# A hybrid RWKV-7 and delta-net block on one core: substitution and half of the low parts on GpSimd, decays from broadcast sums, one inversion list, and a new order

## The chip, the cores and the metric

The kernel runs on one core of one Trainium2 chip. The metric is the device time of one execution in microseconds. The engines are TensorE (PE, with its weight loads listed apart as PEld), VectorE (DVE), ScalarE (ACT), GpSimd (POOL) and SyncE (SP), whose queue issues most of the DMAs; GpSimd issues some too.

## The reference

One layer over 256 latent tokens and 256 context tokens of width 2048: an adaLN-modulated RMSNorm, one input projection `h @ w_in`, two token mixers side by side, a gated merge, an output projection, and a SwiGLU feed-forward part of hidden size 5632. All of it is fp32. What matters here is the two mixers.

The first is a bidirectional RWKV-7 scan of 16 heads of 64. The second is a bidirectional gated delta net of 8 heads of 128, in chunks:

```python
gc = jnp.cumsum(chunks(g), axis=-1)
diff = gc[..., :, None] - gc[..., None, :]
decay = jnp.where(incl, jnp.exp(jnp.where(incl, diff, 0.0)), 0.0)
lmat = jnp.where(strict, jnp.einsum('nbhik,nbhjk->nbhij', kb, kc) * decay, 0.0)
sol = lax.linalg.triangular_solve(lmat, rhs, left_side=True, lower=True, unit_diagonal=True)
qk = jnp.where(incl, jnp.einsum('nbhik,nbhjk->nbhij', qc, kc) * decay, 0.0)
q_dec = qc * jnp.exp(gc)[..., None]
```

`decay` is a matrix of exponentials of differences of running sums, and the triangular solve is done in the kernel by inverting unit triangular blocks. The RWKV scan is brought into the same chunked form, with its own triangular inverse.

## The kernel before

**Products.** Each fp32 weight is split in two parts that TensorE takes at full rate: ScalarE rounds it to a high part (`whi`), VectorE subtracts that from the weight to get the low part (`wlo`), and TensorE forms high x high, high x low and low x high. In the token stage this is done by `cast` and `products` (pieces of 8 row blocks, split in two halves of 4, so each subtraction has 128x512 elements); outside it by `load_w` and `gemm` (L368 the subtraction, L377 to L379 the three products).

**Stages.** First the modulation and the low-rank columns (to about 120 us). Then the token stage, one function per task: the RWKV pairs (`prepare`, `grams`, `inverse`, `values`, `scan`; eight pairs of heads), and the delta-net heads (`begin` once, then for each head `features`, `tokens`, `decays`, `head_grams`, `head_inverse`, `head_scan`). Weight products for features and gates run between them as filler. Then the merge: two projections of both mixers' outputs (`pa`, `pb`, 16 column blocks each), the output projection (`wout`), and the feed-forward part. Through the heads' stage and the merge, rows of the modulation matrix are summed on VectorE as they arrive (`ada_rest`, `scale2`; L1530), their loads issued by GpSimd.

**The inverse.** `invert` inverts blocks of 64. It writes them to DRAM, reads them back as 16x16 blocks, one to a partition, and solves these by substitution: fifteen steps of one multiplication and one addition, each of 15 to 64 elements on 128 partitions (64 for heads), all on the tile `arena` and each dependent on the last. It writes the result to DRAM, reads it back in block form (`T0`, `Tx`), and joins 16 to 32 and 32 to 64 by small products (`pi` tiles).

**The decays.** `decays(h)` multiplies a triangle of ones by the head's `g` on VectorE (`gm`), sums by a product with the strict triangle `aft`, takes the exponential on ScalarE and masks it on GpSimd (`Ed`). A second product, with `ones`, gives the running sum for the query factor.

**The order.** In the token stage the order on TensorE, VectorE, ScalarE and GpSimd is written out by a planner (`Weave`). Each task hands it one instruction or group at a time; the planner takes the one that can start first by its own costs (the `Lane` constants, `LAT`) and, among equals, by `RANK`. `GATES_A` and `GATES_B` say how many gate products may go after each pair and head. Each engine then works strictly in that order. SyncE's queue holds the loads in the order in which they were handed over.

## Time and profile before

| | before |
|---|---|
| median of 3 runs | 2276.34 us (2275.34 to 2285.3) |
| profiled execution | 2291.02 us |
| its span, first to last instruction | 2289.2 us |
| mean granted TensorE clock | 0.978 |
| token stage | about 120 to 1300 us |
| merge and output projection | about 1300 to 1520 us |
| feed-forward part | about 1520 us to the end |

The three runs are not the profiled execution, which took some 13 us longer; times of single instructions come from that one. In the rows that follow, a group is read as line, engine, operation, output and inputs, shape, count, then busy time in us and the mean of one in ns, then idle time of the engine just before it and what ended that. A helper records nearly all instructions of the token stage, so these have one line (L146) and are told apart by their tiles. A duration of TensorE holds an overlap with the next product.

### The profile page before, as it was taken

To read this page: it belongs to the slowest core of one execution; us is meant where nothing else is said; L and a number is where in the kernel's file an instruction comes from. 1 tells how busy PE (TensorE), PEld (TensorE's weight loads), DVE (VectorE), ACT (ScalarE), POOL (GpSimd) and SP (SyncE) were. 2 spreads that over 40 slices of the span, in tenths; PEclk is the share of its full clock that TensorE was granted. 3 is DMA by queue.
4 is the path that set the end of the run, shared out by engine and by line. 5 is a ranking of instruction groups with operands and counts; after the bars stand their busy time and mean duration, and the time that the engine had idled before them with its cause. 6 is when DMAs were issued, how large, how long until landed. Compare 5 with 4: busy or idle time off the path is not lost. (4 is left out here: it accounts for less than half of the span.)

```text
span 2289.2 us, 53997 instructions
## 1 busy us (share of the span) xinstructions
PE 2191.2 (96%) x22584; PEld 1944.7 (85%) x22584; DVE 1566.3 (68%) x3233; ACT 1068.0 (47%) x1894; POOL 115.2 (5%) x185
## 2 busy tenths in 40 slices
PE   7998999999999999999999989899999999999998
PEld 4766587777878778878889888889999999999997
DVE  3446488778888668888899768774656655545444
ACT  3245555444454455444545464443444444444443
POOL 0000000000000010111101040000000000000000
PEclk9999999989999999999999999999999999999999
DMA  9955544344343436455557777854777776566665
GB/s 388 402 143 166 171 119 131 94 104 108 107 118 107 119 106 190 142 165 157 166 160 251 250 280 266 290 194 144 233 240 235 235 231 213 188 184 192 187 188 162
DMA packets 231924, 430.72 MB, mean 188 GB/s; under 512 B 114944, under 2 KB 129152, under 8 KB 227328
## 3 DMA queue, kind: packets, MB, share of 16 engines
q1 hardware_dynamic: 203744, 350.72, 49.9%
q0 software_dynamic: 14112, 51.39, 7.1%
q10 hardware_dynamic: 13824, 25.17, 3.3%
q8 instruction: 177, 2.90, 0.5%
q14 instruction: 67, 0.55, 0.1%
HBM read 401.44 MB, written 25.77 MB: 187 GB/s over the span
## 5 line engine op out<-in xcount | busy, mean ns | idle before, releaser
L368 DVE TENSOR_TENSOR wlo<-wraw,whi 128x1024 fp32r<-128x1024 f32 x328 | 394.1, 1202 | 329.9 <-ACT whi L367 327.0
L367 ACT CAST whi<-wraw 128x1024 fp32r<-128x1024 f32 x328 | 337.6, 1030 | 478.9 <-PE mm L378 429.2
L146 PE MATMUL mm<-hxh,whi 128*128 128x256 f32 (+1 forms) x1376 | 467.5, 340 | 6.2 <-ACT whi L146 6.0
L146 PE MATMUL mm<-hxh,wlo 128*128 128x256 f32 (+1 forms) x1376 | 465.9, 339 | 4.1 <-DVE wlo L146 3.9
L146 PE MATMUL mm<-hxl,whi 128*128 128x256 f32 (+1 forms) x1376 | 465.7, 338 | 0.0
L379 PE MATMUL mm<-hfh,wlo 128*128 128x256 f32 x1344 | 376.1, 280 | 0.5 <-DVE wlo L368 0.5
L377 PE MATMUL mm<-hfh,whi 128*128 128x256 f32 x1344 | 376.1, 280 | 0.0
L378 PE MATMUL mm<-hfl,whi 128*128 128x256 f32 x1344 | 375.9, 280 | 0.0
L146 PEld LDWEIGHTS mm<-hxh,whi 128*128 128x128 f32 x1376 | 264.3, 192 | 33.9 <-ACT whi L146 7.4
L146 PEld LDWEIGHTS mm<-hxh,wlo 128*128 128x128 f32 x1376 | 264.2, 192 | 31.4 <-DVE wlo L146 6.1
L146 PEld LDWEIGHTS mm<-hxl,whi 128*128 128x128 f32 x1376 | 264.0, 192 | 25.9 <-issue 5.4
L146 DVE TENSOR_TENSOR wlo<-wraw,whi 128x512 fp32r<-128x512 f32 x344 | 236.5, 689 | 68.1 <-ACT whi L146 66.3
L146 ACT CAST whi<-wraw 128x512 fp32r<-128x512 f32 x344 | 205.0, 617 | 112.6 <-PE mm L146 79.0
L379 PEld LDWEIGHTS mm<-hfh,wlo 128*128 128x128 f32 x1344 | 253.2, 188 | 0.9 <-DVE wlo L368 0.9
L377 PEld LDWEIGHTS mm<-hfh,whi 128*128 128x128 f32 x1344 | 253.4, 189 | 0.0
L378 PEld LDWEIGHTS mm<-hfl,whi 128*128 128x128 f32 x1344 | 253.2, 188 | 0.0
L146 DVE TENSOR_TENSOR arena<-arena 128x28 f32<-128x28 f32 (+13 forms) x538 | 133.1, 249 | 23.6 <-DMA arena<-scr 10.5
L377 PE MATMUL mm<-za,whi 128*128 128x256 f32 x512 | 143.3, 280 | 0.0
L379 PE MATMUL mm<-za,wlo 128*128 128x256 f32 x512 | 143.2, 280 | 0.0
L378 PE MATMUL mm<-za,whi 128*128 128x256 f32 x512 | 143.2, 280 | 0.0
L378 PEld LDWEIGHTS mm<-za,whi 128*128 128x128 f32 x512 | 96.4, 188 | 0.0
L379 PEld LDWEIGHTS mm<-za,wlo 128*128 128x128 f32 x512 | 96.4, 188 | 0.0
(320 smaller groups left out, 3978.5 us busy)
## 6 DMA issues: line engine op xcount, KB each, us to landing
wraw<-w SPq DMA_DIRECT2D x172, 512.0 KB, 4.1
wraw<-wgu SPq DMA_DIRECT2D x168, 512.0 KB, 4.4
aw<-ada_rest POOLq DMA_DIRECT2D x96, 512.0 KB, 5.2
aw<-ada_first SPq DMA_DIRECT2D x32, 1024.0 KB, 11.2
wraw<-wdn SPq DMA_DIRECT2D x64, 448.0 KB, 3.7
wraw<-wout SPq DMA_DIRECT2D x32, 512.0 KB, 4.8
aw<-ada_gt ACTq DMA_DIRECT2D x64, 256.0 KB, 4.8
wraw<-wdn SPq DMA_DIRECT2D x32, 512.0 KB, 3.7
```

Source lines behind the costliest of these rows:

```text
L146: return Op(self, cost, lambda: getattr(self.engine, name)(out, *a, **k), kind)
L367: S.copy(hi[:, c, :M], raw[:, c, :M])
L368: V.tensor_sub(lo[:, c, :M], raw[:, c, :M], hi[:, c, :M].bitcast(F32))
L377: E.matmul(ps, hi, Xh[:, k, :n], start=first and i == 0, stop=False)
L378: E.matmul(ps, hi, Xl[:, k, :n], start=False, stop=False)
L379: E.matmul(ps, lo, Xh[:, k, :n], start=False, stop=last and i == len(wt) - 1)
```

## The change

1. **Substitution.** All thirty instructions of each of the sixteen substitutions, and the two fills ahead of them, go to GpSimd. The parameter that chose the engine of the fills is gone.
2. **Low parts.** In the token stage the second half of each piece (128x512) is subtracted on GpSimd, the first half on VectorE. In the merge and the output projection (`side`), where a piece was one subtraction of 128x1024 on VectorE, its first 4 row blocks stay there and the rest goes to GpSimd. The feed-forward part stays as it is.
3. **Decays.** `begin` forms the running sums of `g` in both directions by two scans, stores them to DRAM (`grow`) and transposes them (`gct`). `decays` loads one row to all partitions, subtracts the column on GpSimd, bounds the difference by a mask of 0 and -200 on VectorE (`past`, a new constant) and takes the exponential; the query factor is the exponential of the row itself. Its two products are gone.
4. **Inversion list.** For heads, the second small product of the join runs on quarters of 32x32 (`fours`) rather than on blocks of 64x64.
5. **Order.** New `RANK`, `LAT`, `GATES_A`, `GATES_B` and costs of GpSimd's lane.

```diff
-GATES_A, GATES_B = (6, 2, 3, 4, 0, 1, 4, 3), (2, 3, 0, 1, 1, 0, 9, 1)
+GATES_A, GATES_B = (8, 0, 5, 8, 2, 0, 0, 0), (2, 1, 1, 2, 4, 6, 1, 0)
-LAT = dict(dma=2.04, hop=0.255, own=0.092, grp=32, cg=4, turn=0.17)
+LAT = dict(dma=2.76, hop=0.172, own=0.015, grp=32, cg=4, turn=0.132)
-    g = Lane(G, 0.06, 0.0024, LAT["own"])
+    g = gp = Lane(G, 0.17, 0.0019, LAT["own"])
...
+    put("past", np.where(np.concatenate([u <= v, u >= v], 1), 0.0, -200.0))
...
-                V.tensor_sub(lo[:, c, :M], raw[:, c, :M], hi[:, c, :M].bitcast(F32))
+                for en, d in (((V, c),) if side[0] is V else ((V, slice(c.start, c.start + 4)), (G, slice(c.start + 4, c.stop)))):
+                    en.tensor_sub(lo[:, d, :M], raw[:, d, :M], hi[:, d, :M].bitcast(F32))
...
-            yield v.tensor_mul(pr, X[:nb, j + 1:, j:j + 1].to_broadcast([nb, n, m]),
+            yield g.tensor_mul(pr, X[:nb, j + 1:, j:j + 1].to_broadcast([nb, n, m]),
                                TT[:nb, j:j + 1, :m].to_broadcast([nb, n, m]))
-            yield v.tensor_add(TT[:nb, j + 1:, :m], TT[:nb, j + 1:, :m], pr)
+            yield g.tensor_add(TT[:nb, j + 1:, :m], TT[:nb, j + 1:, :m], pr)
...
+        if nu == 16:
+            yield [e.matmul(pv[64 * h:64 * h + 64, 1, u], Tx[64 * h:64 * h + 64, u, :], Qm[64 * h:64 * h + 64, u, :],
+                            start=True, stop=True) for u in range(nu) for h in range(2)]
+        else:
+            yield [e.matmul(pv[r, 1, u], Tx[r, u, b:b + 32], Qm[r, u, :], start=True, stop=True) for h, u, b, r in fours]
...
-                yield v.tensor_sub(lo[:, g], raw[:, g], hi[:, g].bitcast(F32))
+                yield (gp if k else v).tensor_sub(lo[:, g], raw[:, g], hi[:, g].bitcast(F32))
...
+        yield v.tensor_tensor_scan(t0, ones, sp, 0.0, ALU.mult, ALU.add)
+        yield v.tensor_tensor_scan(t1[:, ::-1], ones, sp[:, ::-1], 0.0, ALU.mult, ALU.add)
+        for d, t in enumerate((t0, t1)):
+            for b in range(4):
+                dq(grow[d, :, P * b:P * b + P], t[32 * b:32 * b + 16])
...
-            gm = gs.tile([P, 4, P], F32, tag="gm", name="gm")
-            yield v.tensor_mul(gm, tri[:, d].unsqueeze(1).to_broadcast([P, 4, P]),
-                               gtok[:, :, col:col + 1].to_broadcast([P, 4, P]))
-            gf = gm.rearrange("p b c -> p (b c)")
-            ps = yield pab
-            yield e.matmul(ps, aft[:, d], gf, start=True, stop=True)
+            row = gs.tile([P, 4, P], F32, tag="row", name="row")
+            yield dq(row.rearrange("p b t -> p (b t)"), grow[d, 8 * d + h, :].partition_broadcast(P))
             ed = gs.tile([P, 4, P], F32, tag=f"Ed{d}", name="Ed")
-            yield s.activation(ed.rearrange("p b c -> p (b c)"), ps, AF.Exp)
-            weave.release(pab)
-            yield g.tensor_mul(ed, ed, tri[:, d].unsqueeze(1).to_broadcast([P, 4, P]))
+            yield g.tensor_sub(ed, row, gct[:, :, col:col + 1].to_broadcast([P, 4, P]))
+            yield v.tensor_tensor(ed, ed, past[:, d].unsqueeze(1).to_broadcast([P, 4, P]), ALU.min)
+            yield s.activation(ed.rearrange("p b c -> p (b c)"), ed.rearrange("p b c -> p (b c)"), AF.Exp)
             Ed.append(ed)
...
-            ps = yield pab
-            yield e.matmul(ps[:, :T], ones, gf[:, 0:T], start=True, stop=True)
-            eq = gs.tile([P, T], F32, tag="eq", name="eq")
-            yield s.activation(eq, ps[:, :T], AF.Exp)
-            weave.release(pab)
-            yield v.tensor_mul(o["Qe"][:, d], o["q"], eq)
+        yield v.tensor_mul(o["Qe"][:, 0], o["q"], first)
+        eq = row[:, 0:2].rearrange("p b c -> p (b c)")
+        yield s.activation(eq, eq, AF.Exp)
+        yield v.tensor_mul(o["Qe"][:, 1], o["q"], eq)
...
     scale_next = scale2()
+    side[0] = G
...
+    side[0] = V
     r = rms_scale(x1p, [ssum, sq], T, "rs")
```

Three places show what moves. Before, a head's substitution stands on VectorE. The numbers 64x60, 64x10x6 and so on are its steps; `Vn` and `St` belong to the scan of another head, `wlo` to a weight:

```order
L146 TENSOR_TENSOR arena<-arena 64x55
L146 TENSOR_SCALAR Vn<-s,btok 128x128
L146 TENSOR_TENSOR arena<-arena 64x11x5
L146 TENSOR_SCALAR Vn<-s,btok 128x128
L146 TENSOR_TENSOR arena<-arena 64x60
L146 TENSOR_TENSOR arena<-arena 64x10x6
L146 TENSOR_TENSOR arena<-arena 64x63
```

Now a head's substitution stands on GpSimd, with issues of modulation rows and low parts between its steps:

```order
L147 TENSOR_TENSOR arena<-arena 64x60
L147 TENSOR_TENSOR arena<-arena 64x6x10
L147 TENSOR_TENSOR arena<-arena 64x55
L125 DMA aw<-ada_rest 128x1024
L147 TENSOR_TENSOR arena<-arena 64x5x11
L125 DMA aw<-ada_rest 128x1024
L147 TENSOR_TENSOR arena<-arena 64x48
L125 DMA aw<-ada_rest 128x1024
L147 TENSOR_TENSOR arena<-arena 64x4x12
```

The chain is the same, and what stands between its steps is now GpSimd's other work instead of VectorE's.

On TensorE, in the heads' stage before, a decays' product with ones (`pa<-arena,C 128x256`) stands among the weight products, ahead of the head's Gram products (`pa<-arena 128x128`):

```order
L146 MATMUL pi<-T_12267,LT 32x32 x16
L146 MATMUL mm<-hxh,wlo 128x512
L146 MATMUL pa<-arena,C 128x256
L146 MATMUL mm<-hxh,whi 128x512
L146 MATMUL mm<-hxl,whi 128x512
L146 MATMUL mm<-hxh,wlo 128x512
L146 MATMUL pi<-Tx,qo 32x32 x16
L146 MATMUL mm<-hxh,whi 128x512
L146 MATMUL mm<-hxl,whi 128x512
L146 MATMUL pa<-arena 128x128 x2
```

Now, at the like place of a head, only weight products stand between the inverse's join and the Gram products:

```order
L147 MATMUL pi<-Tx,qo 32x32 x16
L147 MATMUL mm<-hxh,whi 128x256
L147 MATMUL mm<-hxl,whi 128x256
L147 MATMUL mm<-hxh,wlo 128x256
L147 MATMUL mm<-hxh,whi 128x256
L147 MATMUL pa<-arena 128x128 x2
```

Two products of each direction are gone from there.

On GpSimd in the merge, before, the multiplications of the first projection by its gates (L1578) alternate with issues of rows (L1528):

```order
L1555 DMA gts<-gts__1351 128x4x256
L1578 TENSOR_TENSOR PA<-PA,gts 128x256 x6
L1528 DMA aw<-ada_rest 128x1024 x3
L1578 TENSOR_TENSOR PA<-PA,gts 128x256
L1528 DMA aw<-ada_rest 128x1024
L1578 TENSOR_TENSOR PA<-PA,gts 128x256
```

Now (L1590 and L1539 are the same two lines) a low part of each piece stands between them:

```order
L1590 TENSOR_TENSOR PA<-PA,gts 128x256
L1539 DMA aw<-ada_rest 128x1024
L371 TENSOR_TENSOR wlo<-wraw,whi 128x512
L1590 TENSOR_TENSOR PA<-PA,gts 128x256
L1539 DMA aw<-ada_rest 128x1024
L371 TENSOR_TENSOR wlo<-wraw,whi 128x512
```

Each low part waits for its own weight, and what stands behind it on GpSimd waits with it.

More of the change, by code (lines that the diff above doesn't have):

```diff
@@ L561, in unit_rows, with invert @@
         return bass.AP(a.tensor, a.offset + (2 * u0 + h) * UNIT, [[64, 64], [2 * UNIT, nu], [1, 64]])
-    def invert(pool, Lt, parts, nu, which, full, fill):
+    def invert(pool, Lt, parts, nu, which, full):
         h2 = nu // 2
@@ L675, in emit @@
     btok = cst.tile([P, 4, 16], F32, name="btok")
+    gct = cst.tile([P, 4, 16], F32, name="gct")
+    grow = dpool.tile([2, 16, 512], F32, name="grow")
     egc = cst.tile([P, 4, 16], F32, name="egc")
@@ L1163, in begin @@
         sp, bet, t0, t1 = (l2s[:, i:i + P] for i in range(0, 512, P))
[L1164 removed]
+        t2 = gs.tile([P, 512], F32, tag="row", name="t2")[:, 0:P]
         yield dq(sp, abd.rearrange("b r t -> (b r) t"))
@@ L1309, in decays @@
-            eq = gs.tile([P, T], F32, tag="eq", name="eq")
-            yield s.activation(eq, ps[:, :T], AF.Exp)
-            weave.release(pab)
-            yield v.tensor_mul(o["Qe"][:, d], o["q"], eq)
+                first = gs.tile([P, T], F32, tag="eq", name="eq")
+                yield s.activation(first, row[:, 0:2].rearrange("p b c -> p (b c)"), AF.Exp)
+        yield "feat", h
+        yield "scan", NPAIR - 1 if h else NPAIR - 2
+        if h > 1:
+            yield "gscan", h - 2
+        o["Qe"] = gs.tile([P, 2, T], F32, tag="Qe", name="Qe")
```

39 lines of the change are left out of this document (17 added, 22 removed).

## The prediction

> **What bounds the kernel now.** First the page's engines and its chain of waits.
>
> ```profile
> span 2289.2 us, 53997 instructions
> PE 2191.2 (96%) x22584; PEld 1944.7 (85%) x22584; DVE 1566.3 (68%) x3233; ACT 1068.0 (47%) x1894; POOL 115.2 (5%) x185
> PE 38%; DMA 3%; DVE 2%; ACT 1%; issue 1%; POOL 0%; SPq 0%; DVEq 0%; ACTq 0%; POOLq 0%
> ```
>
> TensorE is the bound almost everywhere; GpSimd is nearly empty. The view of stretches shows where that is less true. Its columns are the length, then busy time of PE, weight load, DVE, ACT and POOL, then granted clock, DMA share, GB/s.
>
> ```profile
> 120.00:300.00 180.00, 159.97 (x1348) 115.27 (x1346) 104.14 (x235) 95.13 (x170) 4.47 (x9) 0.93 0.54 158
> 300.00:740.00 440.00, 428.68 (x6203) 350.11 (x6203) 360.90 (x890) 219.52 (x518) 13.70 (x39) 0.96 0.43 112
> 740.00:1300.00 560.00, 544.16 (x5691) 461.18 (x5689) 464.22 (x1192) 279.46 (x564) 56.88 (x83) 1.00 0.56 164
> 1345.00:1395.00 50.00, 41.26 (x316) 38.47 (x314) 45.24 (x52) 28.04 (x46) 21.29 (x24) 0.93 0.92 331
> 1395.00:1520.00 125.00, 116.12 (x942) 113.30 (x939) 99.35 (x130) 58.00 (x74) 6.89 (x13) 0.96 0.77 259
> 1600.00:1700.00 100.00, 100.00 (x860) 100.00 (x859) 60.41 (x89) 42.44 (x54) 0.00 (x0) 1.00 0.74 236
> ```
>
> The change touches 120 to 1520 us: the RWKV pairs to 740, the delta-net heads to 1300, then the two merge projections and the output projection. The feed-forward part behind (a third of the span) keeps its code. From 120 to 1300 TensorE idles 20.0 + 11.3 + 15.8 = 47 us, while VectorE is 82 to 83% busy from 300 on. Only in 1345 to 1395 is VectorE (90%) the fuller one: TensorE idles 8.7 of 50 us there. The last row is TensorE's true pace: 860 products of 256 columns in 100 us, 0.116 us each. Single products are listed at 0.280 us, so a listed duration holds some 0.164 us of overlap with the next product. Who ends TensorE's idle time in 300 to 1300 (total, times, longest):
>
> ```profile
> PE pa L146 <- ACT arena L146: 7.1, 8, 1.3
> PE s L146 <- DVE VX L146: 3.5, 5, 1.9
> PE pa L146 <- DVE LAc L146: 2.9, 1, 2.9
> PE pi L146 <- DVE T L146: 2.7, 2, 1.7
> PE pi L146 <- DVE arena L146: 2.4, 6, 0.8
> PE s L146 <- DVE Y L146: 1.7, 2, 1.5
> ```
>
> Five of the six are VectorE, and each is short: no single wait is worth much, and what counts first is work taken off TensorE.
>
> **The change part by part.** Decays. Per head and direction the fp32 product with the strict mask (512 columns) and the one with ones (256 columns) go. The trace shows each fp32 product as two entries. In the heads' stage:
>
> ```profile
> L146 PE MATMUL pa<-arena,C 128*128 128x512 f32 x48 | 25.8, 618 | 7.1 <-ACT arena L146 7.1
> L146 PE MATMUL pa<-arena,C 128*128 128x256 f32 x48 | 14.6, 386 | 0.0
> L146 PE MATMUL pi<-arena,Tx 64*64 64x16 f32 x320 | 10.9, 208 | 0.7 <-DVE arena L146 0.6
> L146 PE MATMUL pi<-T,LT 32*32 32x16 f32 x512 | 6.3, 180 | 3.0 <-DVE T L146 2.7 <-DMA T<-tscr 0.3
> ```
>
> Of each 48 entries 32 are decays (16 are the key's or the query's l2 norm). By busy time they are 32/48 of 25.8 + 14.6, 26.9 us; by duration less overlap 32 x (0.618 - 0.164) + 32 x (0.386 - 0.164) = 21.6 us. I take **-21.6**, since TensorE's pace and not its listed duration is what others wait for; -26.9 is the far end, 0 the near one (if the heads' inversions, and not TensorE, set the pace; a rival).
>
> In their place stand a broadcast load of 256 KB on SP's queue per direction, a subtraction on GpSimd (where the mask product stood), a minimum on VectorE (where the mask multiplication stood) and the same exponentials on ScalarE. The load may start when the row tile is free, ahead of its head, so I cost it at nothing: the cover is the weight products between two heads. If that cover is gone, it costs about one weight load, a few microseconds, for each direction of the first head. The two scans, two transposes and eight small stores in the setup of the heads stand beside the last pair's scan. The constants grow by 256 columns, 131 KB; the first 120 us move 383 GB/s at a full DMA share, so **+0.3**:
>
> ```profile
> 0.00:120.00 120.00, 104.75 (x1299) 74.52 (x1300) 50.47 (x135) 35.37 (x66) 0.41 (x5) 0.97 1.01 383
> ```
>
> The heads' list: sixteen 64x64 products per head become thirty-two of 32x32 in four quadrants. Of the 320 entries above 256 are these, 256/320 x 10.9 = 8.7 us; 512 entries at 6.3/512 make 6.3. **-2**, between 0 and -4.
>
> VectorE's relief. Off it go half of the token stage's low parts (172 of 344) and the sixteen substitutions, 480 small instructions:
>
> ```profile
> L146 DVE TENSOR_TENSOR wlo<-wraw,whi 128x512 fp32r<-128x512 f32 x344 | 236.5, 689 | 68.1 <-ACT whi L146 66.3
> L146 DVE TENSOR_TENSOR arena<-arena 64x63 f32<-64x63 f32 x32 | 6.9, 215 | 0.9
> L146 DVE TENSOR_TENSOR arena<-arena 64x15 f32<-64x15 f32 x32 | 5.3, 164 | 2.2 <-DMA arena<-scr 1.8
> ```
>
> That is 172 x 0.689 = 118 us and 480 x about 0.195 = 94 us (between the last two rows), 212 of the 929 us that VectorE is busy from 120 to 1300. Its queue gets shorter ahead of every product that waits for it. Of the 47 us idle I take **-14**; 0 if the new order spends it elsewhere, -25 if it ends nearly all waits that name VectorE and the slow start.
>
> The substitution on GpSimd. It is a chain of thirty dependent instructions, and the inversion's products stand in TensorE's fixed order behind it. Today, in two of the heads (first and last small instruction):
>
> ```profile
> 1037.23 0.16 DVE L146 TENSOR_TENSOR arena<-arena 64x15 f32<-64x15 f32 x1
> ...
> 1046.82 1.01 DVE L146 TENSOR_TENSOR arena<-arena 64x39 f32<-64x39 f32 x5
> ...
> 1205.62 0.16 DVE L146 TENSOR_TENSOR arena<-arena 64x15 f32<-64x15 f32 x1
> ...
> 1221.20 0.36 DVE L146 TENSOR_TENSOR arena<-arena 64x15 f32<-64x15 f32 x2
> ```
>
> 10.6 and 15.9 us, of which 30 x 0.195 = 5.8 is the thirty instructions; the rest is other work between them. 13.3 is the middle. On GpSimd the trace has no instruction of this size; the nearest:
>
> ```profile
> L146 POOL MEMSET arena<- 128x16 f32 x8 | 1.0, 126 | 0.5
> L146 DVE MEMSET arena<- 128x16 f32 x8 | 0.6, 72 | 0.0
> L1578 POOL TENSOR_TENSOR PA<-PA,gts x16: 724/1468/3084, 1310.9 to 1370.2; 128x256 f32<-128x256 f32 x16
> 768.84 1.09 POOL L146 TENSOR_TENSOR arena<-arena,C 128x512 f32<-128x512 f32 x1 [39.83 <-ACT arena L146]
> L124 POOL DMA_DIRECT2D aw<-ada_rest x64 | 34.9, 546 | 272.4 <-DVE aw L146 163.3 <-DVE arena L146 46.0 <-ACT aw L146 42.9
> ```
>
> The memsets differ by 0.054 us: 0.195 + 0.054 = 0.25. A line through the shortest 256 (0.724) and the 512 (1.09) gives 0.36 + 0.0014 x 48 = 0.43. I take 0.30, nearer to the memset, whose size is nearest. Thirty make 9.0; the order puts one to three low parts between them (2 x 1.25) and three to five issues of modulation rows (4 x 0.55), and some 1.4 of waiting for the port that the next part is about: 15.1 us. For pairs it is covered: between the last Gram products and the inversion's first, the fourth pair had 46 products of 256 columns and 48 of 512, and now has 96 and 76. For heads the cover hardly grows (60 and 83 become 71 and 89 in the fourth): worth about 1 us beside the decays' products that leave it. So 15.1 - 13.3 - 1 = 0.8 late, eight times: **+6**, between 0 (0.25 each) and +50 (0.43 each).
>
> The Trainium skill's GPSIMD Engine Reference (Performance versus the Vector engine) has about 2.6 cycles per element for two inputs; 2048 elements in 4497 ns leave, by my estimate from it, some 0.06 us fixed, 0.16 us for 48 elements. By that the substitution would be no later than today and the sum 6 us lower; no run here shows the size.
>
> Low parts on GpSimd against VectorE. This is what speaks against the change:
>
> ```profile
> 1310.87 0.73 POOL L1578 TENSOR_TENSOR PA<-PA,gts 128x256 f32<-128x256 f32 x1 [10.60 <-ACT gts L1561]
> 1342.34 1.50 POOL L1578 TENSOR_TENSOR PA<-PA,gts 128x256 f32<-128x256 f32 x1 [0.42 <-ACT PA L1559]
> ...
> 1342.02 1.22 DVE L368 TENSOR_TENSOR wlo<-wraw,whi 128x1024 fp32r<-128x1024 f32 x1 [1.70 <-ACT whi L367]
> 1347.80 1.76 DVE L1530 SCALAR_TENSOR_TENSOR acc<-aw,ck,acc 128x1024 f32<-128x1024 f32 x1
> 1369.99 1.28 DVE L1530 SCALAR_TENSOR_TENSOR acc<-aw,ck,acc 128x1024 f32<-128x1024 f32 x1
> ```
>
> The same multiplication takes 0.73 us alone and 1.50 beside VectorE's subtraction; VectorE's row sum takes 1.28 alone and 1.76 beside GpSimd. Instructions with two SBUF inputs on the two engines nearly exclude each other. The Trainium skill, GPSIMD Engine Reference (Specifications), states such contention for VectorE instructions with two SBUF inputs; by that rule, and the trace agrees (1.50 against 0.73), a half moved is not a half gained.
>
> In the token stage this is room enough: 172 x 1.09 + 480 x 0.30 = 331 us of GpSimd in 1180. In the merge it is not. A piece of eight row blocks costs 1.22 now, and 0.69 + 1.09 = 1.78 of both. In 1345 to 1395 TensorE does about 14 pieces (41.26 us at 24 x 0.116): 14 x 0.55 = 7.7 us more in a stretch that is full. Behind it, 48 pieces add 26 us beside 99.35 us busy of 125: just full. **+9**: the first all of it, the second nearly nothing. Ends: -8 (VectorE's own half is ready 0.5 us sooner, TensorE's idle 8.7 us go) and +29.
>
> The sum: -21.6 + 0.3 - 2 - 14 + 6 + 9 = **-22.3 us**. The profiled span (2289.2) is 13 us over the runs' median of 2276.34; nothing suggests that the difference changes, so 2276.3 - 22.3 = **2254 us**.
>
> **The rivals.** *The heads' inversions set the pace.* At 0.43 us each the substitution takes 12.9 + 2.5 + 2.2 + 2.8 (twice the waiting) = 20.4, 6.1 late per head, 49 us: 2276.3 - 28.3 + 49 = **2297**, slower. It decides from 28.3/8 = 3.5 us late per head, about 0.36 us per instruction. For it: TensorE's order is fixed, and weight products behind the late one can't go ahead; GpSimd's queue now also holds issues that wait for VectorE (163 us today, harmless on an empty engine). Against it: VectorE hands over the transposed blocks sooner.
>
> *The port is the bound in the merge.* With +29 for +9: **2274**. For it: the 50 us at 90%. Against: the modulation rows that fill VectorE there aren't urgent, and can slip towards the feed-forward part.
>
> *More is gained.* -25 for the waits, +2 and +2 for the two costs: **2232**. For it: VectorE falls from 83% to some 65%. Against: waits move in a new order rather than vanish.
>
> **How the numbers follow.** Forecast 0.52 (own range 2242 to 2268), inversions 0.18, port 0.14, more 0.16. A measurement of this kernel tells about 0.5% (11 us) from no change: faster is below 2265, slower above 2287.7. Faster: 0.48 + 0.16 + 0.03 of the port's = 0.67. Slower: 0.15 of the inversions', 0.03 of the port's, 0.01 = 0.19. Same: 0.14. The range runs from the "more" case to the inversions': 2230 to 2298.
>
> **What would show it.** Right: no decay products among TensorE's rows, its idle time in 300 to 1300 below 20 us, no wait over 2 us on the inversion's first product. Wrong: "PE pi" waiting for T or the transposed blocks by tens of us (the small GpSimd instructions are then over 0.36 us); TensorE waiting for GpSimd's low parts in the merge by more than 15 us; or VectorE's 128x512 low part well over 0.69.

## The result and the profile after

The changed kernel takes 2341.8 us (median of four executions, 2338.4 to 2347.3) where the kernel before, run beside it, takes 2278.9: a ratio of 1.0275, with a 95% interval of 1.0242 to 1.0308. It is 63 us slower. The forecast was 2254 us and faster; the range ended at 2298.

The page of the changed kernel, its engines:

```profile
span 2338.1 us, 55005 instructions
PE 2190.0 (94%) x22778; PEld 1944.6 (83%) x22778; DVE 1479.4 (63%) x2569; ACT 1068.1 (46%) x1893; POOL 617.6 (26%) x925
```

VectorE is 87 us less busy, although the halves and the substitutions that left it in the token stage alone took 118 + 94 us there before: most of the rest came back as longer instructions, as a table further down shows. GpSimd is 502 us busier. A single instruction is less than twice as long there (a low part of 128x512 took 0.69 us on VectorE before and takes 1.36 on GpSimd in the mean). TensorE's busy time is as before, and its idle time (span less busy) went from 98.0 to 148.1 us. The view of stretches (columns as in the prediction) shows where:

```profile
120.00:300.00 180.00, 156.44 (x1373) 112.93 (x1372) 94.97 (x174) 92.05 (x166) 45.83 (x62) 0.95 0.52 158
300.00:740.00 440.00, 424.15 (x6314) 338.86 (x6314) 327.39 (x688) 226.67 (x538) 159.50 (x290) 0.98 0.41 108
740.00:1300.00 560.00, 521.67 (x5466) 447.82 (x5463) 384.25 (x768) 266.24 (x528) 252.45 (x436) 0.97 0.54 165
...
1380.00:1570.00 190.00, 164.34 (x1269) 158.15 (x1269) 160.51 (x178) 84.21 (x114) 118.17 (x93) 0.94 0.74 243
```

In 740 to 1300, the heads, VectorE fell from 83 to 69% and TensorE nevertheless idles 38.3 us, where it was 15.8. In the last row, the two merge projections' second half and the output projection, TensorE idles 25.7 of 190 us and VectorE is 84% busy, with half of the low parts gone from it. Of the 47 us by which the first feed-forward product comes later in this execution (1533.6 us before, 1580.9 now), 31 are there when the first product of the merge starts (1300.4 and 1331.6), and 16 are added behind it. The feed-forward part itself takes 756 and 757 us; eight pieces of its weights, loaded during the output projection, are split between the engines too.

The third column from the end, the granted clock of TensorE, moved too: 0.97 in the heads, where it was 1.00. In the traces this clock is either full or one half, and in a half stretch products are slower: in the changed kernel's merge products of 256 columns follow one another every 0.21 us from 1416.3 to 1419.7 us, with the clock at one half, and every 0.116 us ahead of that and behind it. An estimate of what that costs, from the view of stretches in steps of 5 us (TensorE's busy time multiplied by what is missing from the full clock), is 41 us in the kernel before and 52 in the changed one; of this, 2 and 16 us are in the heads, 10 and 18 between 1300 and 1600 us. This is a part of why TensorE's busy time stands still although the decays' products left it. What lowers the clock was not tried.

Who ends TensorE's idle time from 300 to 1330 and, in the second fence, from 1320 to 1560 (total, times, longest):

```profile
PE mm L147 <- POOL wlo L147: 16.2, 9, 2.9
PE mm L147 <- DVE wlo L147: 9.5, 7, 2.8
PE pa L147 <- ACT arena L147: 8.8, 7, 3.6
PE pi L147 <- DVE qo L147: 3.7, 3, 1.3
```

```profile
PE mm L382 <- DVE wlo L371: 20.5, 18, 3.1
PE mm L380 <- ACT whi L369: 6.8, 6, 1.9
```

Before, no low part was among the first six waits of 300 to 1300. Now the two that head the list are low parts (wlo), from GpSimd and from VectorE alike. In the merge TensorE waits for them 20.5 us; in the kernel before the same stretch had this:

```profile
PE mm L379 <- DVE wlo L368: 10.4, 11, 3.5
PE mm L377 <- ACT whi L367: 6.7, 5, 3.5
```

The inversions, which the first rival feared, hardly show: "PE pi" waits for VectorE's qo (3.7 us), not for T.

### The profile page after: what moved, and what is told of

Its sections match the earlier page's. It is cut to its first block, busy times and chain, and to the rows that moved or that the text cites. A ratio compares the mean times of both kernels' runs of the same rounds, so it can differ in the third digit from the quotient of the medians.

```text
span 2338.1 us, 55005 instructions
## 1 busy us (share of the span) xinstructions
PE 2190.0 (94%) x22778; PEld 1944.6 (83%) x22778; DVE 1479.4 (63%) x2569; ACT 1068.1 (46%) x1893; POOL 617.6 (26%) x925
## 4 chain that ended last, share of the span: by engine, by line
PE 41%; DVE 4%; DMA 4%; POOL 3%; issue 2%; ACT 2%; SPq 0%; DVEq 0%; ACTq 0%; POOLq 0%
PE mm L382 12%; PE mm L380 12%; PE mm L381 12%; PE mm L147 2%; POOL arena L147 2%; PE s L147 1%; DMA aw<-ada_rest 1%; DVE wlo L371 1%; POOL wlo L147 1%; DVE arena L147 1%; DVE acc L1541 1%; PE pa L147 1%; DMA wr<-wgu 1%; PE pi L147 1%; DMA wraw<-pa 0%
## 5 line engine op out<-in xcount | busy, mean ns | idle before, releaser
L371 DVE TENSOR_TENSOR wlo<-wraw,whi 128x1024 fp32r<-128x1024 f32 (+1 forms) x328 | 384.7, 1173 | 334.5 <-ACT whi L369 332.1
L147 PE MATMUL mm<-hxh,wlo 128*128 128x256 f32 (+1 forms) x1376 | 470.9, 342 | 31.7 <-POOL wlo L147 17.4
L147 POOL TENSOR_TENSOR wlo<-wraw,whi 128x512 fp32r<-128x512 f32 x172 | 233.3, 1358 | 669.1 <-ACT whi L147 537.6
L147 PEld LDWEIGHTS mm<-hxh,wlo 128*128 128x128 f32 x1376 | 266.6, 194 | 61.4 <-POOL wlo L147 20.5
L147 DVE TENSOR_TENSOR wlo<-wraw,whi 128x512 fp32r<-128x512 f32 x172 | 132.9, 773 | 100.7 <-ACT whi L147 99.6
L147 POOL TENSOR_TENSOR arena<-arena 128x15 f32<-128x15 f32 (+15 forms) x480 | 164.4, 343 | 50.2 <-DMA arena<-scr 16.9
L147 DVE SCALAR_TENSOR_TENSOR aw<-aw,ck 128x512 f32<-128x512 f32 x120 | 106.4, 909 | 23.4 <-DMA aw<-ada_rest 23.2
```

What stands on the lines that cost most here:

```text
L147: return Op(self, cost, lambda: getattr(self.engine, name)(out, *a, **k), kind)
L371: en.tensor_sub(lo[:, d, :M], raw[:, d, :M], hi[:, d, :M].bitcast(F32))
```

## The experiments

Each kernel ran against the kernel before on the same chip. "Order kept" means that the planner still priced an instruction as GpSimd's and placed it there, and only the engine that it was issued on was changed; "planned anew" means that the planner made its own order. The merge is not ordered by the planner; there only the instructions named are changed. Idle is span less TensorE's busy time, from the page of each profiled execution (98.0 for the kernel before).

| run | ratio, 95% interval | TensorE busy / idle, us |
|---|---|---|
| the changed kernel | 1.0275 [1.0242, 1.0308] | 2190.0 / 148.1 |
| low_v | 1.0167 [1.0149, 1.0185] | 2181.9 / 136.7 |
| sub_v | 1.0394 [1.0373, 1.0415] | 2207.9 / 174.3 |
| low_sub_v | 1.0307 [1.0291, 1.0322] | 2194.7 / 154.6 |
| side_v | 1.0156 [1.0128, 1.0184] | 2178.8 / 132.9 |
| low_side_v | 1.0088 [1.0057, 1.0119] | 2172.1 / 131.7 |
| side_v_extra | 1.0362 [1.0336, 1.0387] | 2191.1 / 175.0 |
| old_tables | 1.0303 [1.0258, 1.0348] | 2197.4 / 167.6 |
| new_tables | 1.0224 [1.0179, 1.0269] | 2199.6 / 126.0 |
| decays_list | 1.0023 [1.0001, 1.0044] | 2171.0 / 120.4 |
| no_decay_products | 1.0000 [0.9980, 1.0021] | 2177.1 / 108.6 |
| list_alone | 1.0005 [0.9989, 1.0020] | 2184.2 / 100.1 |
| decays_list_sub_g | 1.0300 [1.0266, 1.0333] | 2197.2 / 159.9 |
| price_decays_list_sub_g | 1.0038 [1.0017, 1.0059] | 2177.5 / 122.5 |
| decays_list_low_g | 1.0289 [1.0260, 1.0319] | 2188.2 / 158.8 |
| pairs_sub_g | 1.0040 [1.0021, 1.0059] | 2178.2 / 118.6 |
| price_pairs_sub_g | 0.9990 [0.9972, 1.0009] | 2173.6 / 113.5 |
| price_low_side_v | 1.0122 [1.0078, 1.0165] | 2177.5 / 132.4 |
| price_after | 1.0236 [1.0201, 1.0271] | 2189.6 / 153.2 |

### One engine at a time, order kept

low_v: the second half of each weight piece's low part, in the token stage, goes back to VectorE.

```diff
-                yield (gp if k else v).tensor_sub(lo[:, g], raw[:, g], hi[:, g].bitcast(F32))
+                o = (gp if k else v).tensor_sub(lo[:, g], raw[:, g], hi[:, g].bitcast(F32))
+                if k:
+                    o.call = lambda a=(lo[:, g], raw[:, g], hi[:, g].bitcast(F32)): V.tensor_sub(*a)
+                yield o
```

> The second half of the token stage's low parts is issued on VectorE again, at the place in the program where the planner put GpSimd's; TensorE's and ScalarE's order up to the merge stays that of the changed kernel. Theory L (GpSimd delivers the low parts late: 1.29 us each against 0.69, in a queue that also holds the substitution's 15 us chains): about 40 us of the 63 go, so 2342 - 40 = 2300, between 2288 and 2312; the merge keeps its loss. Theory S (the substitution on GpSimd, 0.33 us an instruction, makes the inversions late): little changes, 2330 to 2345. Theory O (the new order itself costs the time): 2330 to 2345 as well, or more, since VectorE gets 118 us of work back.

The ratio falls from 1.0275 to 1.0167, 25 us (0.0108 of 2279). Theory L holds in its direction, at 25 instead of 40 and outside its range (2288 to 2312; 25 us less is 2317). The mechanism that it names, a low part that comes late, is not separated here from VectorE's longer instructions.

sub_v: the thirty instructions of each substitution go back to VectorE in the same way.

```diff
-            yield g.tensor_mul(pr, X[:nb, j + 1:, j:j + 1].to_broadcast([nb, n, m]),
-                               TT[:nb, j:j + 1, :m].to_broadcast([nb, n, m]))
-            yield g.tensor_add(TT[:nb, j + 1:, :m], TT[:nb, j + 1:, :m], pr)
+            a = (pr, X[:nb, j + 1:, j:j + 1].to_broadcast([nb, n, m]), TT[:nb, j:j + 1, :m].to_broadcast([nb, n, m]))
+            o = g.tensor_mul(*a)
+            o.call = lambda a=a: V.tensor_mul(*a)
+            yield o
...
```

> The 480 instructions of the substitution are issued on VectorE again, at the place where the planner put GpSimd's; the low parts stay halved, and the order of TensorE and ScalarE up to the merge stays. Theory S: the heads' period falls from 62 to about 56 us, 2342 - 45 = 2297. Theory L in the form that a low part is late because it stands behind a chain in GpSimd's queue: some 20 to 30 us go, 2312 to 2322. Theory L in the form that a GpSimd low part is late by its own 1.29 us: under 10 us, 2332 or more. Theory O: 2335 to 2350.

It is slower than the changed kernel by 0.0119, 27 us, beyond every range that was named. Theory S falls in this order: taking the substitution away from GpSimd costs. The order was made with it there, so this does not say what the substitution costs in an order of its own; decays_list_sub_g and its successor do.

low_sub_v: both edits.

> Both are issued on VectorE, in the same order of the program: what is left of the change is the decays, the heads' list, GpSimd's half of the merge's low parts, and the order. Theories L and S: TensorE's idle time before 1300 us is back near the 47 us of before and the decays' 22 us are gained, so 2342 - 65 = 2277 (2265 to 2290), with the merge's loss of some 18 us still in it. Theory O: 2320 or more, for the order is the changed kernel's.

1.0307: what low_v gains, the substitution on VectorE loses again and a little more. That is in theory O's range. But the order was made with the substitution off VectorE, and this run can't tell the order from the load on VectorE; the runs with the tables below bear on it.

side_v: the merge's low parts go back to VectorE whole.

```diff
-    side[0] = G
```

> Only the merge's low parts go back to VectorE whole; all else is the changed kernel. If the half on GpSimd is what the merge lost (15 to 18 us between the last inversion and the first feed-forward product, TensorE's waits for wlo 20.5 against 10.4 us), 2342 - 16 = 2326 (2318 to 2334). If VectorE would have been full there anyway, within 5 us of 2342.

1.0156, 27 us less than the changed kernel: the merge's loss is the halves on GpSimd, and it is larger than the 16 that the waits let expect.

low_side_v: low_v and side_v together.

> The token stage's second halves of the low parts (same place in the program) and the merge's low parts are on VectorE; the substitution stays on GpSimd. Low_v took 25 us off the changed kernel's 1.0275 and side_v 27, by their ratios. If the two losses are separate, as their places in time say, the ratio is 1.0275 - 0.0108 - 0.0119 = 1.005, 2290 where the kernel before takes 2279. If one frees what the other needed (a shared backlog), 1.010 or more. That it stays above 1 while the decays left TensorE would mean that something else, the order, still costs some 30 us.

1.0088, between the two forecasts: the sum of the two gains would give 1.005. So the halves are 43 us of the 63, and 20 us of the loss remain with no low part on GpSimd, though the decays' products are gone from TensorE. TensorE's busy time is 18 us shorter than in the changed kernel with the same products in it: by the estimate of above the half clock costs 30 us here and 52 there, which covers it.

### Why a half on GpSimd is not a half gained

One piece of the merge in the changed kernel's timeline (start, duration, engine, line, operation; TensorE's and ScalarE's rows are left out):

```profile
1419.65 0.42 DVE L386 TENSOR_TENSOR ml<-arena,mh 128x256 fp32r<-128x256 f32 x1
...
1420.12 0.69 DVE L371 TENSOR_TENSOR wlo<-wraw,whi 128x512 fp32r<-128x512 f32 x1
...
1420.18 1.79 POOL L371 TENSOR_TENSOR wlo<-wraw,whi 128x512 fp32r<-128x512 f32 x1 [2.86 <-ACT whi L369]
...
1420.73 1.52 DVE L386 TENSOR_TENSOR ml<-arena,mh 128x256 fp32r<-128x256 f32 x1
```

VectorE's half runs its 0.69 us from 1420.12 to 1420.81. GpSimd's begins beside it at 1420.18 and takes 1.79; undisturbed it takes 1.27 (the shortest of its row), so it did nothing until some 1420.70, about when VectorE ended. VectorE's next instruction takes 1.52 us, to 1422.25, for what took 0.42 in the first row, and GpSimd ended at 1421.97: it waited for nearly all of it. In these rows the instructions exclude each other for nearly their whole length. The Trainium skill's SBUF — State Buffer (Who interferes with whom) states this of a VectorE instruction with two SBUF inputs beside a GpSimd one that reads SBUF: a lock, not a share of bandwidth. The trace agrees, with 1.52 against 0.42. So a piece that took VectorE 1.22 us takes the two 0.69 + 1.27 = 1.96 of a port that only one can have.

The same is seen over the whole token stage. VectorE's rows with both inputs in SBUF are longer in the changed kernel, and those with an input in PSUM (the tiles `pa` and `s`, which TensorE writes) are not:

| VectorE's row | inputs | mean before, us | mean in the changed kernel, us |
|---|---|---|---|
| aw<-aw,ck 128x512 | SBUF | 0.751 | 0.909 |
| LAl<-arena 64x256 | SBUF | 0.414 | 0.561 |
| acc<-aw,ck,acc 128x1024 (heads and merge) | SBUF | 1.356 | 1.650 |
| LAl<-pa,C 64x512 | one in PSUM | 0.688 | 0.688 |
| VX<-s,et 64x128 | one in PSUM | 0.286 | 0.287 |

That the port and not the late half costs the time needed an experiment. side_v_extra leaves the low parts whole on VectorE, and gives GpSimd beside each a subtraction of the same size that nothing waits for (`extra` is a tile of 512 columns):

```diff
+                if extra[0] is not None and c.stop - c.start == 8:
+                    G.tensor_sub(extra[0], hi[:, c.start + 4:c.stop, :M].bitcast(F32).rearrange('p k m -> p (k m)'), C[:, 0:512])
...
-    side[0] = G
+    extra[0] = gp.tile([P, 512], F32, name="extra")
...
```

> As side_v (the merge's low parts whole on VectorE), and beside each of them GpSimd does a subtraction of two SBUF inputs of 128x512 whose result nothing reads: the load on the shared port without the product's wait for GpSimd. Theory P (the port: each engine slows the other, as the prediction had it): VectorE's 1.22 us piece goes to 1.5 to 1.9 us and the 27 us that side_v gained are lost again or more, ratio 1.024 or above. Theory W (lateness: the product waits for the slower engine, 1.68 us for its half where VectorE does the whole in 1.22): VectorE's piece stays near 1.22, ratio near side_v's 1.0156, under 1.019.

1.0362 against side_v's 1.0156: 47 us for an operation that no product waits for. VectorE's groups from 1320 to 1560 in side_v, and then in side_v_extra (busy us, mean ns, idle before):

```profile
L371 DVE TENSOR_TENSOR wlo<-wraw,whi 128x1024 fp32r<-128x1024 f32 x66 | 80.7, 1225 | 23.2 <-ACT whi L369 22.2
L1592 DVE TENSOR_TENSOR arena<-arena,PA 128x256 f32<-128x256 f32 x16 | 6.7, 421 | 0.9
```

```profile
L373 DVE TENSOR_TENSOR wlo<-wraw,whi 128x1024 fp32r<-128x1024 f32 x52 | 80.4, 1555 | 13.3 <-ACT whi L369 13.2
L1596 DVE TENSOR_TENSOR arena<-arena,PA 128x256 f32<-128x256 f32 x16 | 18.5, 1162 | 1.4
L371 POOL TENSOR_TENSOR extra<-whi,C 128x512 f32<-128x512 f32 x52 | 85.5, 1644 | 58.7 <-ACT whi L369 57.7
```

The same subtraction on VectorE goes from 1.23 to 1.56 us in the mean, the sum with PA from 0.42 to 1.16. TensorE's waits for VectorE's low part go from 11.1 us to 30.3 in this stretch, those for ScalarE's high part from 5.7 to 7.8. Theory P holds. One part of the 47 us may be of another kind: the unread subtraction reads `whi` and so holds its buffer, and ScalarE waited 10.8 us for GpSimd before it could write the next. In the changed kernel the halves in this stretch were these, on VectorE and on GpSimd:

```profile
L371 DVE TENSOR_TENSOR wlo<-wraw,whi 128x512 fp32r<-128x512 f32 x60 | 65.8, 1098 | 23.7 <-ACT whi L369 23.7
...
L371 POOL TENSOR_TENSOR wlo<-wraw,whi 128x512 fp32r<-128x512 f32 x60 | 94.7, 1579 | 36.8 <-ACT whi L369 32.8 <-DVE arena L1593 3.4
```

VectorE's half costs 1.10 where the whole cost 1.22 to 1.24: a tenth was gained, not a half.

### TensorE's time in the heads

decays_list: the kernel before with the decays from broadcast rows and the heads' list, its own tables, VectorE for the substitutions and all low parts.

> The kernel before with the decays from broadcast rows and the heads' list alone: its tables, substitution and low parts stay before's (VectorE). The sum of those terms was -21.6 + 0.3 - 2: ratio 0.990, 2255 against 2279. By the trace of the changed kernel, in which these products' rows hold 25 us less, 0.989. If the heads are paced by the inversions and not by TensorE, 0.998 to 1.002. If the broadcast rows on SP's queue come late or the planner makes a worse order of it, above 1.00.

1.0023: nothing is gained. TensorE's busy time did fall by 20.2 us, and its idle time rose by 22.4. To see whether the new code or the new order takes it back, no_decay_products keeps the kernel before and its order, and only cuts the decays' products to 16 columns, so that the decays' values are left out.

```diff
-            yield e.matmul(ps, aft[:, d], gf, start=True, stop=True)
+            op = e.matmul(ps, aft[:, d], gf, start=True, stop=True)
+            op.call = lambda a=(ps[:, :16], aft[:, d], gf[:, :16]): E.matmul(*a, start=True, stop=True)
+            yield op
...
-            yield e.matmul(ps[:, :T], ones, gf[:, 0:T], start=True, stop=True)
+            op = e.matmul(ps[:, :T], ones, gf[:, 0:T], start=True, stop=True)
+            op.call = lambda a=(ps[:, :16], ones, gf[:, 0:16]): E.matmul(*a, start=True, stop=True)
+            yield op
```

> The kernel before, its order kept on every engine, with the decays' two fp32 products per head and direction cut from 512 and 256 columns to 16 (the exponentials read those 16 again and again); the decays' values are left out of the computation by this. Theory T (TensorE's time is the pace of the heads, as the prediction had it): -18 to -22 us, ratio 0.990 to 0.992. Theory D (TensorE's time is not the pace; what is taken off it comes back as waits for VectorE and the inversions): within 5 us, 0.998 to 1.002.

1.0000, between 0.998 and 1.0021: theory D. TensorE is 14.1 us less busy over the span, and 10.6 us more idle. The heads' stage here (its row before stands in the prediction):

```profile
740.00:1300.00 560.00, 537.13 (x5712) 460.48 (x5707) 466.86 (x1197) 279.85 (x570) 57.28 (x83) 0.99 0.56 167
```

TensorE has 537.13 where it had 544.16, with 21 more products in the window, and VectorE is as full as it was (466.86, 83%). Waits of TensorE in this stretch:

```profile
PE pa L146 <- ACT arena L146: 7.1, 8, 1.3
PE pi L146 <- DVE arena L146: 5.1, 8, 2.2
PE s L146 <- DVE Vn L146: 2.1, 5, 1.1
```

"PE pi" for VectorE's arena was 1.1 us in the same 740 to 1300 of the kernel before, "PE s" for Vn 0.6. What TensorE no longer does, it waits, for the most part; a part comes back in the clock, which is 0.99 in this row for 1.00 (by the estimate of above 6 us for 2). The waits suggest that a chain through the inversions, the scans and VectorE sets the pace of the heads. No run shortened that chain alone, so this is not shown. It is not VectorE's load alone: price_decays_list_sub_g, further down, takes 77 us off VectorE and is not faster either.

list_alone: the kernel before with the heads' list alone.

> The kernel before with the heads' list alone, planned anew with its own tables. By the rows of TensorE the list takes 7 us off the heads (64x64 x16 rows of 30.7 us go to 18.4 + 5.6). If TensorE's time there is not the pace, as no_decay_products shows for the decays, it comes back as waits: 0.998 to 1.002. If it is gained in full: 0.997.

1.0005 [0.9989, 1.0020]. TensorE is 7.0 us less busy, the time is not less. The list's own share of the 7 is 3: in the heads its row of 10.9 us (x320) became 2.0 (x64) and 5.8 (x512). The expectation compared rows of the whole kernel, in which the pairs' products, which the list leaves alone, have become shorter too (0.214 us for 0.222 in the mean), at a granted clock of 0.981 for 0.978.

### The order, and the price that it is planned with

The planner makes a fixed order from prices. For GpSimd's small instructions of 40 columns it had 0.16 us before the change, 0.25 after; the changed kernel's trace has this:

```profile
L147 POOL TENSOR_TENSOR arena<-arena 64x63 f32<-64x63 f32 x32 | 10.8, 337 | 1.9
L147 POOL TENSOR_TENSOR arena<-arena 64x39 f32<-64x39 f32 x32 | 10.3, 321 | 2.2
```

decays_list_sub_g: decays_list with the substitution on GpSimd at the price of before (the two lines of the substitution on `g`, tables of before).

> Decays_list (1.0023) and the substitution on GpSimd, low parts on VectorE, tables of before, with the planner free to make its order for it. Theory S (the heads' inversions get late): 1.01 or more. Theory R (VectorE, 83% busy, is relieved of 94 us that were in the way of TensorE): 0.985 to 0.997. low_side_v is the same with the new tables, at 1.0088; the difference is the tables' alone.

1.0300: theory S. Here the rival of the prediction, the late inversions, is seen. TensorE's waits from 740 to 1330:

```profile
PE pi L147 <- DMA T<-tscr: 30.7, 13, 8.4
PE pi L147 <- DVE T L147: 8.0, 7, 2.8
```

price_decays_list_sub_g changes one line, the price:

```diff
-    g = gp = Lane(G, 0.06, 0.0024, LAT["own"])
+    g = gp = Lane(G, 0.27, 0.0020, LAT["own"])
```

> Decays_list_sub_g (1.030, with 31 us of TensorE's waits for T's DMA in the heads) with the true price in the planner and nothing else. Theory Pr: the waits for T shrink to under 10 us and the ratio falls to 1.005 or lower. Theory E: 1.025 or more.

1.0038, and the wait is gone (740 to 1320):

```profile
PE pi L147 <- DVE arena L147: 5.7, 6, 2.4
...
PE pi L147 <- DMA T<-tscr: 4.2, 2, 3.8
```

Of the 63 us that the substitution on GpSimd cost against decays_list, 60 were a fixed order that put the products where the substitution was not done yet. In the two profiled executions 37 of them are idle time of TensorE (159.9 for 122.5), and 20 are busy time of the same products: by the estimate of above the half clock costs 68 us in the first and 48 in the second. Theory Pr holds for this order. With the right price the substitution costs 0.0015 against decays_list, within both intervals.

pairs_sub_g and price_pairs_sub_g: the substitution on GpSimd for the pairs alone, at the price of before and at the true one.

> Decays_list (1.0023) and the substitution on GpSimd for the eight pairs alone, where TensorE has products to do meanwhile; the heads' stays on VectorE. A candidate for the best mix: 0.985 to 0.998 if VectorE's relief counts in the pairs (some 10 us) and the heads lose nothing. Against decays_list_sub_g it tells what the heads' half costs: if that is 10 us or more slower than this one, theory S holds for the heads.

> Pairs_sub_g (1.004) with the true price of GpSimd in the planner: decays from rows, the heads' list, the pairs' substitution on GpSimd, tables of before. The best mix that is left. If VectorE's relief in the pairs was spoiled by the plan alone: 0.990 to 0.998. If TensorE's order is paced by more than these (no_decay_products gained nothing for the decays' products either): 1.000 to 1.005.

1.0040 and 0.9990 [0.9972, 1.0009], the latter between its two ranges. The heads' half was what cost in decays_list_sub_g (1.0300 against 1.0040). The last is the best mix that ran, and is not told from the kernel before.

decays_list_low_g: decays_list with the token stage's halves on GpSimd, substitution on VectorE, tables of before. The price of a low part, 0.06 + 0.0024 x 512 = 1.29 us, was right here.

> Decays_list (1.0023) and the second halves of the token stage's low parts on GpSimd, the substitution on VectorE, tables of before. Theory L (a low part from GpSimd is late by its own 1.29 us against 0.69): 1.01 to 1.02. If only the queue shared with the substitution makes them late: 0.99 to 1.003.

1.0289: worse than theory L's range, and without any substitution in GpSimd's queue. The lateness that theory L names is the smaller part. TensorE's waits from 740 to 1330 name VectorE's results more than GpSimd's low parts:

```profile
PE s L147 <- DVE Vn L147: 10.9, 10, 2.6
PE pi L147 <- DVE arena L147: 6.2, 9, 2.1
PE mm L147 <- POOL wlo L147: 4.3, 2, 3.4
```

The kernel before had 0.6 and 1.1 us for the first two from 740 to 1300. In the changed kernel, where the substitution shares the queue, the waits for GpSimd's low parts were 16.2 us, so there both play a part. What the halves do to VectorE beside them is seen at the substitution's small instructions in the heads, first before, then here:

```profile
L146 DVE TENSOR_TENSOR arena<-arena 64x63 f32<-64x63 f32 x32 | 6.9, 215 | 0.9
L146 DVE TENSOR_TENSOR arena<-arena 64x48 f32<-64x48 f32 x32 | 6.3, 195 | 0.6
```

```profile
L147 DVE TENSOR_TENSOR arena<-arena 64x63 f32<-64x63 f32 x28 | 9.4, 336 | 0.5
L147 DVE TENSOR_TENSOR arena<-arena 64x48 f32<-64x48 f32 x28 | 8.4, 300 | 0.5
```

They are half as long again, as two-input instructions beside GpSimd's are in the merge.

new_tables: the kernel before with the three new tables alone.

> The kernel before with nothing but the three new tables. Theory O: slower by some 30 us, ratio 1.013 or more. Theory E: between 0.99 and 1.005.

1.0224, 51 us (between 41 and 61), in theory O's range. old_tables: the changed kernel with the tables of before. The edit is the three lines of `GATES_A` and `GATES_B`, `RANK` and `LAT`, put in or taken back.

> The changed kernel with the three tables of before (the gates' distribution, the ranks, the latencies); engines, decays and list as changed. Theory O (the new tables are bad by themselves, some 30 us of the loss): 2342 - 30 = 2312 or lower. Theory E (the engines are what costs, and the new tables were the better ones for them): 2342 or slower. The merge's 27 us are in it in both.

1.0303, no better than 1.0275 (the intervals overlap), on theory E's side. So the new tables are worse for the engines of before, the old ones are not better for the changed engines, and this pair does not price the new ones for the changed engines.

price_low_side_v: low_side_v's engines, planned as such, and the true price; price_after: the changed kernel with the true price.

> The changed kernel with all low parts planned and issued on VectorE, and with GpSimd's price in the planner set to what the trace shows (0.27 + 0.0020 us per column: 0.35 us for 40 columns, where the changed kernel has 0.25 and the kernel before 0.16). Low_side_v, planned with the too low price and a half of the low parts on another engine, is at 1.0088. Theory Pr (the fixed order puts the products where the planner thought the substitution would be done, so a wrong price is what costs): 0.995 or lower. Theory E (the engine's own speed costs, whatever the order): 1.005 to 1.012.

> The changed kernel with the true price of GpSimd in the planner (a low part 1.29 us for the planned 1.14, a substitution's instruction 0.35 for 0.25); all engines as changed, the merge's 27 us still in it. Theory Pr: 1.017 or lower, since the 25 us of low parts were late only by the plan. Theory E: 1.024 to 1.031.

Theory Pr falls for the new tables: 1.0122 and 1.0236 where the low price had 1.0088 and 1.0275, both with intervals that overlap. But price_low_side_v differs from price_decays_list_sub_g in the tables alone: 1.0122 [1.0078, 1.0165] against 1.0038 [1.0017, 1.0059], 19 us (between 8 and 30 by the two intervals). The heads' stage of the first and of the second:

```profile
740.00:1300.00 560.00, 511.75 (x5374) 436.90 (x5370) 402.25 (x855) 260.81 (x529) 152.80 (x354) 0.96 0.53 161
```

```profile
740.00:1300.00 560.00, 528.96 (x5611) 453.05 (x5610) 420.09 (x899) 272.68 (x553) 153.90 (x368) 0.97 0.56 172
```

TensorE idles 48.3 us with the new tables and 31.0 with the old, at nearly the same clock. Which entries of the tables do it was not tried.

## Why the prediction was wrong

**TensorE as the pace.** The step "what counts first is work taken off TensorE" failed. The terms for the decays and the list, -21.6 and -2, were sized about rightly as work: decays_list has 20.2 us less of TensorE's busy time, and the list's own rows fell by 3. They are worth 0 in the time of the kernel, in three runs: the interval of decays_list begins at 1.0001, no_decay_products' at 0.998, list_alone's at 0.9989, so a gain of more than 5 us is excluded in each. The prediction had 0 as the near end of the range of the decays and named the reason, that something else sets the pace; it chose the other end, with TensorE 97% busy. Such a share says that little idle time is left to lose, not that work taken away is gained. What does set the pace of the heads stays open.

**VectorE's relief.** "Of the 47 us idle I take -14" failed as well. In the changed kernel VectorE falls from 83 to 69% in the heads, and TensorE's idle time there grows from 15.8 to 38.3 us. The sign named for it, under 20 us of idle time in 300 to 1300, came out at 15.9 + 38.3. The relief doesn't come even without low parts on GpSimd: in price_decays_list_sub_g VectorE is 75% busy in the heads, and TensorE idles 31.0 us there.

**The port in the token stage.** The term counted 172 x 0.689 us off VectorE and nothing for what comes back through the port. The sentence "this is room enough: 331 us of GpSimd in 1180" asked whether GpSimd has time; the question was how long VectorE is shut out. 172 halves at 1.27 us are 218 us of the port for the 118 that left. Measured, the halves cost 25 us in the changed kernel's order and 61 (0.0266 of 2287) in the old one. How much of it is the port and how much the later low part was separated only in the merge.

**The merge's port.** The mechanism was right and the size was not: +9 was taken, 27 us measured, next to the far end of +29, for which the prediction shows no working (its own 7.7 and 26 are 34). The term took the stretch behind 1395 as "just full" and charged nearly nothing for it. VectorE's half was expected at 0.69 and costs 1.10, GpSimd's at 1.09 and costs 1.58. The sign that the prediction named, VectorE's 128x512 low part "well over 0.69", is there; the other, TensorE waiting for GpSimd's low parts by over 15 us, is there for VectorE's (20.5).

**The substitution.** Thirty instructions were priced at 0.30 us and take 0.30 to 0.37 in the heads. The term of +6 is not contradicted: 0.0015 or 3 us with the right price in the planner, between runs whose intervals overlap. The rival of the late inversions is real in an order that was planned with the wrong price (30.7 us of waits). In the changed kernel TensorE does not wait for T, so it is not the cause there. That rival had the direction right, for another reason; its 2297 is 45 us short of the result.

**The order.** The sum had no term for the tables. They cost 19 us where they can be compared with all else the same, and 51 on the kernel before.

| term | taken, us | measured, us | by |
|---|---|---|---|
| decays and list | -23.6 | 0 | decays_list, no_decay_products, list_alone |
| VectorE's relief and the substitution | -14 + 6 | +3 | price_decays_list_sub_g |
| halves in the token stage | 0 | +25 | low_v |
| halves in the merge | +9 | +27 | side_v |
| tables | 0 | +19 | price_low_side_v |

In the second row a relief and a cost may cancel; the run shows them together only. The measured terms add to 74 us for a result of 63. They do not add exactly, as low_side_v shows: its two halves together gave 43, not 52. The 20 us that low_side_v is slower than the kernel before are about the size of the tables' 19, which were measured with another price and order.

## What to carry to other kernels

Before work with two SBUF inputs is moved from VectorE to GpSimd, add up the port and not the engines: where the two meet, the moved instruction's time on GpSimd is charged to VectorE's own two-input instructions as well (here a piece of 1.23 us on VectorE took 1.56 beside an unread subtraction on GpSimd). Where an engine is 97% busy and another 83%, cut the first one's work in the old order, as no_decay_products does, before writing the code that saves it; it takes one edit, and told here that 14 us less of TensorE's busy time were worth nothing. Where a planner fixes the order, measure an operation's duration on its new engine before its price is set: a price of 0.16 us for an instruction that takes 0.33 cost 60 us here. And compare TensorE's busy time of two runs only with the granted clock beside it: 20 of these 60 us were the same products at a lower clock.

## What the runs showed of the hardware that was not expected

A GpSimd low part of 128x512 took 1.27 us in the merge and 1.25 in the token stage when undisturbed (the shortest of each row), where the rows of before had 1.09 for a multiplication of that size. The changed kernel's heads have both sizes of cost beside each other, the low part and the decays' subtraction, whose output is not rounded and whose second input is a broadcast:

```profile
L147 POOL TENSOR_TENSOR wlo<-wraw,whi 128x512 fp32r<-128x512 f32 x91 | 120.1, 1321 | 208.3 <-ACT whi L147 176.5 <-DVE arena L147 11.2 <-DVE Tx L147 6.2
...
L147 POOL TENSOR_TENSOR arena<-arena,gct 128x512 f32<-128x512 f32 x16 | 17.0, 1061 | 31.6 <-DMA arena<-grow 27.9 <-DVE PT L147 3.7
```

1.32 against 1.06 us in the mean, and 1.25 against 1.04 for the shortest of each; whether the output's type or the second read is the reason was not tried. And a GpSimd instruction whose result nobody reads can cost more than one whose result is needed: side_v_extra's 64 unread subtractions, and 8 beside the feed-forward weights, cost 47 us over side_v, 20 more than the halves did. There VectorE keeps the whole piece, so the two engines ask more of the port.
